# Two products at a time, token block by token block, where x is renewed, with other first loads and the first rotary on VectorE

## The chip, the cores and the metric

The kernel runs on one NeuronCore of a Trainium2 chip. TensorE multiplies into PSUM; VectorE, ScalarE and GpSimd do the rest; SyncE issues most DMAs, and ScalarE and GpSimd can issue some too. Each engine works through its own queue in program order and waits on semaphores. The metric is the device time of one execution in microseconds, the median of several runs.

## The reference, cut to what matters

Four layers run one after the other on the same x of 256 tokens by 1024 channels, all in float32: two layers of a first kind and then two of a second kind.

```python
def hybrid_layer(x, ...):             # layers one and two
    hdn = rms_norm(x, norm_w)
    qa, ka, va, za, qb, kb, vb, zb, ga, gb = split_cols(hdn @ w_in)   # 10 x 1024 columns
    ya = dilated_mixture(rope(qa), rope(ka), va) * silu(za)
    yb = rms_norm(diff_attention(rope(qb), rope(kb), vb)) * silu(zb)
    merged = sigmoid(ga) * (ya @ w_proj_a) + sigmoid(gb) * (yb @ w_proj_b)
    return x + merged @ w_out

x = rms_norm(x, final_norm_w)         # between layers two and three

def hybrid_layer_2(x, ...):           # layers three and four
    proj = rmsnorm(x, pre_mix_g) @ w_in
    ...                               # gated delta rule, windowed attention, two gates
    x = x + rmsnorm(mix, post_mix_g)
    ff = square(relu(rmsnorm(x, pre_mlp_g) @ w_ff1)) @ w_ff2
    return x + rmsnorm(ff, post_mlp_g)
```

## The kernel before

Tokens lie on partitions in two token blocks of 128 (`t` = 0, 1), channels in 8 blocks of 128 (`c`). A product of x with a weight of 512 columns needs x transposed: `to_lh` transposes four channel blocks on TensorE (tile `tp`), ScalarE copies them times the norm's gain into the high part `lhi`, and VectorE subtracts this from the product to make the low part `llo`. A weight comes in pieces of two channel blocks (`raw`, 128 x 1024 values, 512 KB): ScalarE copies it to the high part `hi` and VectorE makes the low part `lo` (`split_next`, lines 284 and 285). `mm3` then multiplies high by high, high by low and low by high: three matmuls for one channel block and one token block.

`proj` runs a product of 512 columns: by default channel block by channel block, both token blocks in turn; with `sweep=True` all 8 channel blocks for token block 0 and then all for token block 1, which keeps four pieces alive. `proj_w` is the same with the weight as the stationary side.

All weight pieces stand in one list in order of use (`stream`, filled by `plan1` and `plan2`). `raw` has three buffers (`NRAW`) and `hi` and `lo` four each (`NSPLIT`). `feed` splits the next piece when one of the four is released (`release`, after its last matmul) and asks for the load of the next raw piece behind it. The loads are issued by SyncE; a load waits there until VectorE has made the low part of the piece that had the buffer.

The order on every engine is written out by hand with a clock: one unit of `clk` is two calls of `mm3`. After each `mm3`, `tick(0.5)` calls `feed`, moves the clock on and issues what is due; `at(k, fn)` puts work off by k units. So a number such as the lag of `normed` says behind which matmul an instruction stands.

x is renewed at the end of each layer. In layers one and two this is the product with `w_out`, two column halves (`g` = 0, 1), both with `sweep=True`: `out_evac` adds the result to x (line 805). After layer two it also makes both norms at once (the final norm and the next layer's first): squares on ScalarE, the fold with the final gain on VectorE (line 816), factors on GpSimd (`both`), then `normed` (line 583) and `to_lh`; `own` scales x itself. In layers three and four the second matrix of the MLP adds up 8 blocks `fc` of the hidden width in PSUM (`back`); the last block goes token block by token block, and `post` and `update` (lines 857 to 873) make the norm, add to x and call `then`, which norms x for the next layer. The layers of the second kind begin with a gate of 512 columns (`silu_gate(0, True)`) and a small product of 272 columns (`small`), whose pieces are 128 x 544.

At the start x and the first pieces are loaded, the first gain is turned into columns (`norm_columns`), and `prepare` transposes x for layer one. `turned` copies query or key tiles out of PSUM, turns 16 of every 64 columns (`rope`, four instructions on GpSimd, lines 427 to 430) and `flip` transposes the tile.

## Time and profile before

| | |
|---|---|
| median of 3 runs | 1742.82 us (1741.65 to 1745.22) |
| profiled execution, its own time | 1741.27 us |
| its span, first to last instruction | 1739.5 us |
| TensorE busy | 1705.6 us, 98% |
| VectorE busy | 1169.9 us, 67% |
| ScalarE busy | 996.4 us, 57% |
| GpSimd busy | 268.1 us, 15% |
| read from HBM | 270.53 MB, 156 GB/s over the span |

PE is TensorE's matmuls, PEld its weight loads, DVE VectorE, ACT ScalarE, POOL GpSimd, SP SyncE; a q behind an engine's name means its sequencer, which issues DMAs. A tile is named by what is written and what is read (`lo<-raw,hi`). The duration of one matmul covers its pipeline, so the next one starts before it ends: rows that name several matmuls tell the pace better. PEclk is the share of TensorE's full clock that was granted. In a row of a stretch the last two numbers are the share of time in which the 16 DMA engines were busy and the GB/s that they moved.

### The profile page before, as it was taken

The page shows a single profiled execution, that of the slowest core. Times are in us where ns is not written, and L with a number is a line of the kernel's source. Part 1 is how long each engine was busy: PE and PEld are TensorE (multiplying, and loading weights), DVE is VectorE, ACT ScalarE, POOL GpSimd, SP SyncE. Part 2 cuts the span into 40 slices and gives each one's busy share as a digit, 9 for nine tenths or more (in the row PEclk, how much of TensorE's full clock was granted, in tenths as well). Part 3 has the DMA queues.
Part 4 walks back from the last instruction along what each step waited for, and adds up shares of the span by engine and source line. Part 5 has one row for each costly group of instructions (what it writes and reads, how often), then busy time and mean ns, then how long its engine had stood idle before and what let it go on. Part 6 is the DMA issues. An engine that isn't in the chain of part 4 may idle for free.

```text
span 1739.5 us, 26865 instructions
## 1 busy us (share of the span) xinstructions
PE 1705.6 (98%) x9865; PEld 1484.6 (85%) x9865; DVE 1169.9 (67%) x2189; ACT 996.4 (57%) x1786; POOL 268.1 (15%) x507
## 2 busy tenths in 40 slices
PE   8999999999999999999999999999999999999998
PEld 6788888888888888898889889998998888889997
DVE  5676776666777766788585676555788584775554
ACT  6666665466666654665665455445565666464443
POOL 2112321031123200320220000000320210010000
PEclk9999999999999999999999999999999999999999
DMA  6655465466655565554332655665554333646564
GB/s 206 196 173 167 152 189 173 159 195 181 177 164 155 172 192 174 168 166 134 96 104 86 197 167 182 194 193 170 160 170 140 87 102 93 198 158 195 184 184 140
DMA packets 158932, 282.27 MB, mean 162 GB/s; under 512 B 20560, under 2 KB 28496, under 8 KB 158800
## 3 DMA queue, kind: packets, MB, share of 16 engines
q1 hardware_dynamic: 157840, 277.83, 53.0%
q0 software_dynamic: 720, 2.62, 0.4%
q8 instruction: 78, 1.28, 0.3%
q14 instruction: 54, 0.44, 0.1%
q10 hardware_dynamic: 240, 0.09, 0.0%
HBM read 270.53 MB, written 1.59 MB: 156 GB/s over the span
## 4 chain that ended last, share of the span: by engine, by line
PE 51%; DVE 5%; issue 1%; ACT 1%; POOL 0%; DMA 0%; DVEq 0%; POOLq 0%; SPq 0%; ACTq 0%
PE acc L314 6%; PE acc L312 6%; PE acc L313 6%; PE acc L353 5%; PE acc L354 5%; PE acc L355 5%; PE facc L313 3%; PE facc L312 3%; PE facc L314 3%; DVE lo L285 2%; DVE hcv L993 1%; PE inv L1177 1%; PE inv L1167 1%; PE tp L371 1%; PE pt L507 1%
## 5 line engine op out<-in xcount | busy, mean ns | idle before, releaser
L285 DVE TENSOR_TENSOR lo<-raw,hi 128x1024 fp32r<-128x1024 f32 (+1 forms) x504 | 617.3, 1231 | 343.9 <-ACT hi L284 328.1
L284 ACT ACTIVATE hi<-raw 128x1024 fp32r<-128x1024 f32 (+1 forms) x504 | 527.3, 1052 | 357.5 <-PE acc L314 149.0
L312 PE MATMUL acc<-hi,lhi 128*128 128x512 f32 (+1 forms) x1344 | 550.4, 410 | 1.2 <-ACT lhi L385 1.2
L314 PE MATMUL acc<-hi,llo 128*128 128x512 f32 (+1 forms) x1344 | 526.2, 392 | 0.4 <-DVE llo L388 0.3
L313 PE MATMUL acc<-lo,lhi 128*128 128x512 f32 (+1 forms) x1344 | 524.2, 390 | 0.6 <-DVE lo L285 0.5
L314 PEld LDWEIGHTS acc<-hi,llo 128*128 128x128 f32 x1344 | 253.5, 189 | 57.4 <-DVE llo L388 3.4
L313 PEld LDWEIGHTS acc<-lo,lhi 128*128 128x128 f32 x1344 | 255.3, 190 | 41.3 <-DVE lo L285 2.0
L312 PEld LDWEIGHTS acc<-hi,lhi 128*128 128x128 f32 x1344 | 255.0, 190 | 39.7 <-ACT lhi L385 1.4
L353 PE MATMUL acc<-lhi,hi 128*128 128x256 f32 x832 | 239.1, 287 | 0.0
L355 PE MATMUL acc<-lhi,lo 128*128 128x256 f32 x832 | 235.4, 283 | 0.0
L354 PE MATMUL acc<-llo,hi 128*128 128x256 f32 x832 | 235.4, 283 | 0.0
L353 PEld LDWEIGHTS acc<-lhi,hi 128*128 128x128 f32 x832 | 159.5, 192 | 1.2 <-issue 0.4
L354 PEld LDWEIGHTS acc<-llo,hi 128*128 128x128 f32 x832 | 159.5, 192 | 0.7
L355 PEld LDWEIGHTS acc<-lhi,lo 128*128 128x128 f32 x832 | 159.4, 192 | 0.0
L312 PE MATMUL facc<-hi,fh 128*128 128x512 f32 x256 | 99.8, 390 | 0.0
L313 PE MATMUL facc<-lo,fh 128*128 128x512 f32 x256 | 99.8, 390 | 0.0
L314 PE MATMUL facc<-hi,fl 128*128 128x512 f32 x256 | 99.6, 389 | 0.0
L509 ACT ACTIVATE ptS<-pt 128x384 f32<-128x384 f32 x80 | 39.2, 490 | 82.0 <-PE pt L507 81.8
L546 POOL TENSOR_SCALAR pf<-pss 128x1 f32<-128x1 f32 x8 | 3.7, 458 | 467.6 <-ACT pj L860 467.6
L500 DVE CUSTOM_DVE_ANT_0 s<-sc,tab 128x256 f32<-128x256 f32 x192 | 60.4, 352 | 11.2 <-PE sc L496 10.6
L993 DVE SCALAR_TENSOR_TENSOR hcv<-acc,cw,hcv 128x255 f32<-128x255 f32 (+1 forms) x144 | 58.2, 475 | 1.5 <-ACT hcv L990 1.4
L314 PEld LDWEIGHTS facc<-hi,fl 128*128 128x128 f32 x256 | 48.1, 188 | 10.1
(306 smaller groups left out, 2206.9 us busy)
## 6 DMA issues: line engine op xcount, KB each, us to landing
raw<-in_w_in_dram SPq DMA_DIRECT2D x272, 512.0 KB, 3.8
raw<-in_w_ff_dram SPq DMA_DIRECT2D x128, 512.0 KB, 4.4
raw<-in_w_proj_a_dram SPq DMA_DIRECT2D x16, 512.0 KB, 3.9
raw<-in_w_proj_b_dram SPq DMA_DIRECT2D x16, 512.0 KB, 3.7
raw<-in_w_out_dram SPq DMA_DIRECT2D x16, 512.0 KB, 3.7
raw<-in_w_up_sw_dram SPq DMA_DIRECT2D x16, 512.0 KB, 3.7
raw<-in_w_up_dn_dram SPq DMA_DIRECT2D x16, 512.0 KB, 3.7
raw<-in_w_o_dram SPq DMA_DIRECT2D x16, 512.0 KB, 3.8
```

The costliest lines, as they stand in the source:

```text
L284: S.activation(hi[:, :, :o], raw[:, :, :o], AF.Copy)
L285: V.tensor_tensor(out=lo[:, :, :o], in0=raw[:, :, :o], in1=hi[:, :, :o].bitcast(F32), op=ALU.subtract)
L312: T.matmul(a, lh[0][:, c, sl], hi[:, cc, :n], start=first, stop=False)
L313: T.matmul(a, lh[0][:, c, sl], lo[:, cc, :n], start=False, stop=False)
L314: T.matmul(a, lh[1][:, c, sl], hi[:, cc, :n], start=False, stop=last)
L353: T.matmul(a, hi[:, c % 2, sl], lh[0][:, c, :], start=(c == 0 and m % 2 == 0), stop=False)
L354: T.matmul(a, hi[:, c % 2, sl], lh[1][:, c, :], start=False, stop=False)
L355: T.matmul(a, lo[:, c % 2, sl], lh[0][:, c, :], start=False, stop=(c == 7 and m % 2 == 1))
L371: T.transpose(p[:, a, :], src[:, a * 128:(a + 1) * 128], ident)
L500: V.tensor_tensor_reduce(s[:, a:b], sc[:, a:b], bias[:, a:b], 1.0, FMIN, ALU.add, ALU.max, accum_out=mx[:, j:j + 1])
L509: S.activation(r, pt, AF.Copy)
L993: V.scalar_tensor_tensor(ha[:, m, d:], a[:, m, :256 - d], tap(3 - d, m), ha[:, m, d:], op0=ALU.mult, op1=ALU.add)
```

## The change

1. `proj_pair` runs two products at a time: all channel blocks of both for token block 0, then of both for token block 1. It serves the two halves of the output product of layer two, and the gate and the small product at the start of layers three and four. The last two blocks of the MLP's second matrix run in the same way (`back_last`).
2. Eight pieces are alive in such a pair, so four of them get a place of their own (`HOMES`): tiles of other stages that are free then. A piece with such a home doesn't count against the four `hi` and `lo` buffers; `feed` leaves at least `PACE` = 1.4 clock units between two splits when three pieces already wait.
3. The lags of `normed` go from 1.8 to 3.2 and 3.6 (layer two) and from 1.1 to 3.5 and 4.2 (layer three), and two calls of `pump` at the ends of these layers go.
4. At the start the second half of the first token block is loaded from ScalarE's queue, the first piece in two loads, and seven pieces are asked for at once, four of them into tiles of later stages. The first x columns are transposed ahead of the first split, and the first piece is split in halves.
5. The rotary of the first query and key tiles of layer one goes to VectorE.

```diff
+PACE = 1.4
+HOMES = {1: ("qk", "qk", "tok", "R"), 2: ("qk", "qk", "tok", "tg")}
...
-    def x_load(t, h=None):
+    def x_load(t, h=None, queue=nc.sync):
         c = slice(0, DM) if h is None else slice(512 * h, 512 * h + 512)
-        nc.sync.dma_start(X[:, t, c], I["x"][0, t * 128:(t + 1) * 128, c])
+        queue.dma_start(X[:, t, c], I["x"][0, t * 128:(t + 1) * 128, c])
...
-    count = {"raw": 0, "split": 0, "done": 0, "free": 0}
-    def plan(W, *segs):
+    count = {"raw": 0, "split": 0, "own": 0, "done": 0, "free": 0, "at": -9.0}
+    owns = deque()
+    def plan(W, *segs, homes=(None,) * 4):
         for k in range(0, 8, 2):
-            stream.append((W, k, segs))
-    def load_next():
-        W, k0, segs = stream[count["raw"]]
+            stream.append((W, k, segs, homes[k // 2]))
+    def load_next(home=None, rows_apart=False):
+        W, k0, segs, _ = stream[count["raw"]]
         count["raw"] += 1
-        raw = wp.tile([128, 2, 512], F32, name="raw", tag="raw", bufs=NRAW)
+        if home is None:
+            raw = wp.tile([128, 2, 512], F32, name="raw", tag="raw", bufs=NRAW)
+        else:
+            raw = act.tile([128, 2, 512], F32, name="raw", tag=home, bufs=2)
         o = 0
         for c0, n in segs:
-            nc.sync.dma_start(raw[:, :, o:o + n],
-                              W[k0 * 128:(k0 + 2) * 128, c0:c0 + n].rearrange("(c p) n -> p c n", p=128))
+            for c in ((0, 1), (1, 2)) if rows_apart else ((0, 2),):
+                nc.sync.dma_start(raw[:, c[0]:c[1], o:o + n],
+                                  W[(k0 + c[0]) * 128:(k0 + c[1]) * 128, c0:c0 + n].rearrange("(c p) n -> p c n", p=128))
             o += n
         raws.append((raw, o))
 
-    def split_next():
+    def split_next(rows_apart=False):
         raw, o = raws.popleft()
+        home = stream[count["split"]][3]
         count["split"] += 1
-        hi = wp.tile([128, 2, 512], F32R, name="hi", tag="hi", bufs=NSPLIT)
-        lo = wp.tile([128, 2, 512], F32R, name="lo", tag="lo", bufs=NSPLIT)
-        S.activation(hi[:, :, :o], raw[:, :, :o], AF.Copy)
-        V.tensor_tensor(out=lo[:, :, :o], in0=raw[:, :, :o], in1=hi[:, :, :o].bitcast(F32), op=ALU.subtract)
+        count["at"] = clk[0]
+        owns.append(home is None)
+        if home is None:
+            count["own"] += 1
+            hi = wp.tile([128, 2, 512], F32R, name="hi", tag="hi", bufs=NSPLIT)
+            lo = wp.tile([128, 2, 512], F32R, name="lo", tag="lo", bufs=NSPLIT)
+        elif home == "qk":
+            both = act.tile([128, 2, 2, 512], F32R, name="hl", tag="qk", bufs=2)
+            hi, lo = both[:, 0], both[:, 1]
+        else:
+            hi, lo = [act.tile([128, 2, 512], F32R, name=n, tag=home, bufs=2) for n in ("hi", "lo")]
+        for c in (slice(0, 1), slice(1, 2)) if rows_apart else (slice(0, 2),):
+            S.activation(hi[:, c, :o], raw[:, c, :o], AF.Copy)
+            V.tensor_tensor(out=lo[:, c, :o], in0=raw[:, c, :o], in1=hi[:, c, :o].bitcast(F32), op=ALU.subtract)
...
-        while count["split"] < len(stream) and count["split"] < count["free"] + NSPLIT:
+        while count["split"] < len(stream):
+            if stream[count["split"]][3] is None:
+                if count["own"] >= count["free"] + NSPLIT:
+                    break
+            if len(splits) >= NSPLIT - 1 and clk[0] - count["at"] < PACE:
+                break
...
-        count["done"] += 1
+        count["done"] += owns.popleft()
...
+    def proj_pair(lh, evacs):
+        accs, pieces = [acc2() for _ in evacs], {}
+        for t in range(2):
+            for j, evac in enumerate(evacs):
+                for c in range(8):
+                    if t == 0 and c % 2 == 0:
+                        pieces[j, c // 2] = piece()
+                    hi, lo, n = pieces[j, c // 2]
+                    mm3(accs[j][t], n, lh, c, t, hi, lo, c % 2, c == 0, c == 7)
+                    if t and c % 2:
+                        release()
+                    if c == 7:
+                        evac(accs[j][t], t)
+                    tick(0.5)
...
-        G.tensor_tensor(out=a, in0=x[:, :, 0:16], in1=tbl(cc, 0, 16), op=ALU.mult)
-        G.tensor_tensor(out=b[:, :, 0:8], in0=x[:, :, 8:16], in1=tbl(ss, 0, 8), op=ALU.mult)
-        G.tensor_tensor(out=b[:, :, 8:16], in0=x[:, :, 0:8], in1=tbl(ss, 8, 16), op=ALU.mult)
-        G.tensor_tensor(out=x[:, :, 0:16], in0=a, in1=b, op=ALU.add)
+        E.tensor_tensor(out=a, in0=x[:, :, 0:16], in1=tbl(cc, 0, 16), op=ALU.mult)
...
             for g in range(2):
-                plan(A, (base + 512 * g, 512))
+                homes = HOMES[1] if l == DEPTH - 1 and g == 0 and A.tensor is I["w_out"].tensor else (None,) * 4
+                plan(A, (base + 512 * g, 512), homes=homes)
     def plan2(l):
         W = I["w_in_2"][l]
         plan(W, (3072, 512))
-        plan(W, (4096, 16), (5136, 256))
+        plan(W, (4096, 16), (5136, 256), homes=HOMES[2])
...
         for fc in range(8):
-            for k, g in ((0, 0), (0, 1), (2, 0), (2, 1)) if fc < 7 else ((0, 0), (2, 0), (0, 1), (2, 1)):
-                stream.append((W2, 4 * fc + k, ((512 * g, 512),)))
+            for i, (k, g) in enumerate(((0, 0), (0, 1), (2, 0), (2, 1)) if fc < 6 else ((0, 0), (2, 0), (0, 1), (2, 1))):
+                stream.append((W2, 4 * fc + k, ((512 * g, 512),), HOMES[2][i] if fc == 6 else None))
...
             q, k = qk_tile([8, 256], F32R), {}
-            proj(lh, into_stack(q, r, rope1)[1], sweep=first)
-            proj(lh, into_keys(k, r, rope1))
+            E = V if first and l == 0 else G
+            proj(lh, into_stack(q, r, rope1, E)[1], sweep=first)
+            proj(lh, into_keys(k, r, rope1, E))
...
                     c = vcol["pre_mix_g_2"]
-                    normed(t, rn, vT[:, c:c + 8], 1.8, xf)
+                    normed(t, rn, vT[:, c:c + 8], (3.2, 3.6)[t], xf)
...
-        for g in range(2):
-            proj(lm, out_evac(g), sweep=True)
-        if l == DEPTH - 1 and not last:
-            pump(clk[0] + 0.3)
+        if l < DEPTH - 1:
+            for g in range(2):
+                proj(lm, out_evac(g), sweep=True)
+        else:
+            proj_pair(lm, [out_evac(g) for g in range(2)])
...
-        def silu_gate(g, sweep=False):
+        def silu_gate(g):
             szs.append(t4k("sz"))
-            proj(lh, into_silu(szs[g], None, dnng[:, 128 * l:128 * l + 128]), sweep=sweep)
-        silu_gate(0, True)
-        proj(lh, small)
+            proj(lh, into_silu(szs[g], None, dnng[:, 128 * l:128 * l + 128]))
+        szs.append(t4k("sz"))
+        proj_pair(lh, [into_silu(szs[0], None, dnng[:, 128 * l:128 * l + 128]), small])
...
-            if fc < 7:
-                for pc in range(2):
-                    for g in range(2):
-                        hi, lo, n = piece()
-                        for cc in range(2):
-                            c = 2 * pc + cc
-                            for t in range(2):
-                                mm3(facc[t][g], 512, (fh, fl), c, t, hi, lo, cc, fc == 0 and c == 0, False)
-                                if t and cc:
-                                    release()
-                                tick(0.5)
-                return
+            for pc in range(2):
+                for g in range(2):
+                    hi, lo, n = piece()
+                    for cc in range(2):
+                        c = 2 * pc + cc
+                        for t in range(2):
+                            mm3(facc[t][g], 512, (fh, fl), c, t, hi, lo, cc, fc == 0 and c == 0, False)
+                            if t and cc:
+                                release()
+                            tick(0.5)
+        def back_last(facc):
             pieces = {}
             for t in range(2):
-                for g in range(2):
-                    for c in range(4):
-                        if t == 0 and c % 2 == 0:
-                            pieces[g, c // 2] = piece()
-                        hi, lo, n = pieces[g, c // 2]
-                        mm3(facc[t][g], 512, (fh, fl), c, t, hi, lo, c % 2, False, c == 3)
-                        if t and c % 2:
-                            release()
-                        if c == 3:
-                            post(facc[t], g, t, fss, gmlp, then, r2)
-                        tick(0.5)
+                for fc in (6, 7):
+                    for g in range(2):
+                        for c in range(4):
+                            if t == 0 and c % 2 == 0:
+                                pieces[fc, g, c // 2] = piece()
+                            hi, lo, n = pieces[fc, g, c // 2]
+                            mm3(facc[t][g], 512, hs[fc], c, t, hi, lo, c % 2, False, fc == 7 and c == 3)
+                            if t and c % 2:
+                                release()
+                            if fc == 7 and c == 3:
+                                post(facc[t], g, t, fss, gmlp, then, r2)
+                            tick(0.5)
...
                     rstd(rn[:, t:t + 1], nss[:, 2 * t:2 * t + 1], nss[:, 2 * t + 1:2 * t + 2])
-                    normed(t, rn[:, t:t + 1], vT[:, c:c + 8], 1.1)
+                    normed(t, rn[:, t:t + 1], vT[:, c:c + 8], (3.5, 4.2)[t])
...
-        for fc in range(8):
+        for fc in range(6):
             back(fc, facc)
-            if fc + 2 < 8:
-                hidden(fc + 2)
-        if not last:
-            pump(clk[0] + 0.9)
+            hidden(fc + 2)
+        back_last(facc)
...
+    x_load(0, 1, nc.scalar)
     norm_columns = column_load("norm_w")
-    x_load(0, 1)
-    load_next()
+    load_next(rows_apart=True)
...
-    load_next()
-    norm_columns()
-    split_next()
     x_load(1)
     load_next()
-    for t in range(2):
-        at(0.7 * t, lambda t=t: prepare(t, vT[:, vcol["norm_w"]:vcol["norm_w"] + 8], lag=2.6))
-    pump(0)
+    for home in ("sz", "sz", "tg", "tg"):
+        load_next(home)
+    norm_columns()
+    gain = vT[:, vcol["norm_w"]:vcol["norm_w"] + 8]
+    prepare(0, gain, (0,), 2.2)
+    split_next(rows_apart=True)
+    split_next()
+    prepare(0, gain, (1,), 2.3)
+    at(1.2, lambda: prepare(1, gain, lag=2.6))
     feed()
     tab_load("cc", "if")
     at(1.8, lambda: tab_load("ca", "ba"))
```

## Rows read from the trace of the kernel before

**Rows 1.** The page, part 1: busy time of TensorE, share of the span, instructions.

```profile
PE 1705.6 (98%) x9865; PEld 1484.6 (85%) x9865; DVE 1169.9 (67%) x2189; ACT 996.4 (57%) x1786; POOL 268.1 (15%) x507
```

**Rows 2.** List of waits, TensorE, whole trace: who, for whom, total us, times, longest.

```profile
PE tp L446 <- POOL tok L430: 4.0, 2, 3.6
```

**Rows 3.** List of waits, TensorE, from 698 to 712 us.

```profile
PE tp L371 <- DVE xn L583: 1.3, 2, 0.6
PE tp L371 <- DVE xf L583: 0.9, 1, 0.9
```

**Rows 4.** List of waits, TensorE, from 1214 to 1228 us.

```profile
PE tp L371 <- DVE xn L583: 3.1, 2, 1.9
```

**Rows 5.** Stretches: length; busy us of PE, PEld, DVE, ACT, POOL; clock; DMA share.

```profile
5.00:9.10 4.10, 2.43 (x12) 1.76 (x13) 1.94 (x5) 2.85 (x9) 0.00 (x0) 1.00 1.02 380
...
26.16:29.58 3.42, 3.42 (x10) 2.65 (x9) 1.51 (x3) 2.48 (x4) 1.01 (x3) 0.50 0.77 294
29.58:60.00 30.42, 28.79 (x134) 23.03 (x133) 20.14 (x46) 18.05 (x24) 5.58 (x10) 1.00 0.67 187
...
698.00:712.00 14.00, 11.85 (x58) 8.78 (x57) 12.07 (x26) 9.22 (x25) 4.50 (x8) 1.00 0.39 98
...
1217.40:1220.80 3.40, 3.40 (x12) 2.67 (x13) 3.31 (x8) 2.47 (x9) 1.99 (x2) 0.50 0.54 110
```

**Rows 6.** Timeline, TensorE, start: start us, us, instruction, idle before and releaser.

```profile
7.61 0.51 PE L312 MATMUL acc<-hi,lhi 128*128 128x512 f32 x1 [1.18 <-ACT lhi L385]
...
21.15 0.39 PE L314 MATMUL acc<-hi,llo 128*128 128x512 f32 x1
```

**Rows 7.** Timeline, GpSimd and VectorE around the first rotary.

```profile
18.39 0.24 POOL L569 TENSOR_SCALAR rstd<-root 128x1 f32<-128x1 f32 x1
...
20.33 3.75 DVE L285 TENSOR_TENSOR lo<-raw,hi 128x1024 fp32r<-128x1024 f32 x3 [3.03 <-ACT hi L284]
...
21.68 1.32 POOL L427 TENSOR_TENSOR ra<-tok,tab 128x128 f32<-128x128 f32 x1
...
28.54 0.46 POOL L427 TENSOR_TENSOR ra<-tok,tab 128x128 f32<-128x128 f32 x1 [3.48 <-ACT tok L440]
```

**Rows 8.** Groups by line, VectorE, 0 to 60 us: busy us, mean ns.

```profile
L164 DVE SCALAR_TENSOR_TENSOR lv<-lv 128x64 f32<-128x64 f32 x4 | 0.7, 221 | 0.0
```

**Rows 9.** Groups by line, VectorE, from 684 to 722 us.

```profile
L285 DVE TENSOR_TENSOR lo<-raw,hi 128x1024 fp32r<-128x1024 f32 x9 | 10.9, 1224 | 4.1 <-ACT hi L284 4.1
L388 DVE SCALAR_TENSOR_TENSOR llo<-tp,vT,lhi 128x128 fp32r<-128x128 f32 x16 | 4.5, 347 | 0.2 <-ACT lhi L385 0.2
...
L805 DVE TENSOR_TENSOR X<-acc,X 128x512 f32<-128x512 f32 x4 | 2.8, 688 | 1.5 <-PE acc L314 1.5
...
L583 DVE TENSOR_SCALAR xn<-X,rr 128x512 f32<-128x512 f32 x2 | 1.0, 484 | 0.9 <-POOL rr L547 0.9
```

**Rows 10.** Groups by line, ScalarE, from 684 to 722 us.

```profile
L284 ACT ACTIVATE hi<-raw 128x1024 fp32r<-128x1024 f32 x10 | 10.4, 1057 | 4.1 <-DMA raw<-in_w_out_dram 2.2 <-DMA raw<-in_w_in_dram 1.8
...
L540 ACT ACTIVATE junk<-X 128x512 f32<-128x512 f32 x6 | 3.8, 629 | 4.4 <-DVE X L805 3.1 <-DVE X L816 1.3
L284 ACT ACTIVATE hi<-raw 128x544 fp32r<-128x544 f32 x4 | 2.6, 659 | 2.4 <-PE acc L314 1.6 <-DMA raw<-in_w_in_dram 0.9
```

**Rows 11.** Timeline, VectorE and TensorE, second gated product of layer two.

```profile
668.07 1.22 DVE L285 TENSOR_TENSOR lo<-raw,hi 128x1024 fp32r<-128x1024 f32 x1
...
675.48 0.60 PE L371 MATMUL tp<-ident,tg 128*128 128x128 f32 x4
```

**Rows 12.** DMA issues, 700 to 709 us: count, KB each, us to landing.

```profile
raw<-in_w_in_dram SPq DMA_DIRECT2D x3, 256.0 KB, 3.1
raw<-in_w_in_dram SPq DMA_DIRECT2D x1, 512.0 KB, 3.9
```

**Rows 13.** Timeline, VectorE, splits of the small product's weights.

```profile
715.95 0.72 DVE L285 TENSOR_TENSOR lo<-raw,hi 128x544 fp32r<-128x544 f32 x1 [0.63 <-ACT hi L284]
...
718.78 3.00 DVE L285 TENSOR_TENSOR lo<-raw,hi 128x544 fp32r<-128x544 f32 x2
```

17 lines of the change are left out of this document (10 added, 7 removed).

## The prediction

> **What bounds the kernel now.** I read the page first: TensorE is busy 98% of the span [rows 1]. A change can therefore win only the moments in which TensorE stands still or runs slowly, and must not make new ones. The list of TensorE's waits says where they are. Two of its largest entries lie at the places that the change touches: 3.6 us for the first rotary product [rows 2], and the transposes that wait for the normed x, 2.2 us between layers two and three [rows 3] and 3.1 us between layers three and four [rows 4]. Next I cut the trace into stretches. After the 3.6 us wait TensorE was granted half its clock (1.2 instead of 2.4 GHz) for 3.4 us, and again at 1217.4 us, behind the longer wait of [rows 4]. At half clock 10 instructions took 3.42 us; the 134 of the next stretch took 28.8 us of busy time, 0.215 each, so the 10 would have needed 2.15 [rows 5]: a slow stretch costs about 1.3 us. Then I read the timelines around the four places, and in the passages the duration of each kind of VectorE instruction, because weights, gates and norms all pass through VectorE.
>
> **Start (first loads, first rotary).** TensorE idles 1.2 us before its first real product, which ends at 21.4 us [rows 6]; at the first flip of the query tile it idles the 3.6. The flip is late because the four rotary instructions run on GpSimd: the first takes 1.32 us while VectorE splits three weights from 20.33 us on, and only 0.46 later, beside an idle VectorE [rows 7]. VectorE has no such instruction of 128 elements here; the nearest are 0.22 us for 64 elements [rows 8] and 0.69 for 512 [rows 9]. Four cost between 0.9 and 2.8 us; I take 1.0, near the 64-element row. The change gives them to VectorE for the first query and key tiles of layer one. There they wait for ScalarE's copy, and behind them in VectorE's queue stands the low part of the next product's first weight, for which TensorE waits. I follow it: the factor is ready at 18.6 in the trace [rows 7], 17.7 if the start is 0.9 earlier (below); the copy of 512 columns and two squares take about 0.7 + 2 x 0.8, the high part 1.06 [rows 10], the low part 1.2 [rows 9]: 22.3. The first product then ends at 20.5, one set of transposes later it is 21.1 and the first matmul that needs no low part is over at 21.3. So the flip no longer waits (3.6 us and the slow stretch of 1.3 go) and 1.0 us comes back.
>
> The loads: seven weight pieces are asked for at once instead of three and then one for each freed buffer; the second half of x goes by ScalarE's queue, behind the identity; SyncE's queue is short of that issue and has the second token block ahead of the third weight. The DMA engines run full there anyway (share 1.02 from 5 to 9.1 us [rows 5]), so the other queue gets nothing. The rotary table is issued behind four more pieces; at the 380 GB/s of that stretch seven pieces of 0.52 MB and x are in by about 16 us, before the rotary at 18.4. What remains is that ScalarE copies the first x columns ahead of the first weight, which it now takes in halves: bounds 0 and the 1.2 of [rows 6]; I take 0.9, since the weight's 1.06 us stood ahead of all columns. Start: -3.6 - 1.3 + 1.0 - 0.9 = -4.8 us, bounds -6.1 and -2.6.
>
> **Layers two to three (684 to 720 us).** After the change both column halves of the output product run for token block 0, then for block 1, and the next layer does the same with its gate and its small product. x of block 0 is complete 10.3 us (48 matmuls of 0.215) before the layer ends instead of 5.2. But the split of the next weights is tied to buffers: the gate's four pieces may be split only as the second half's pieces are released, in the last 5.2 us, just where VectorE has block 0's norm too. I lay out its queue from the first release (time 0, 18 matmuls or 3.9 us before the layer's end) with the durations of [rows 9]: from 0.2 the fold of the previous half 0.69, two normings 0.96, a split 1.2, eight low copies 2.25, two splits 2.4, block 0's own scaling about 0.48 + 0.69, the last addition 0.69, its fold 0.69, the fourth split 1.2. That ends at 11.4. TensorE wants it at 9.7: 3.9 of the old layer, two sets of transposes at 0.6 [rows 11], six of eight blocks of the gate (3.9) and 0.7 of waiting for the first norming. A wait of 1.7 us. Behind it comes the ring of three raw tiles: the small product's third piece needs the tile that the gate's fourth frees at 11.4; its load is issued in two parts, and the larger lands 3.1 us after its issue [rows 12], not before 14.5; high part 0.66 [rows 10], low part 0.72 [rows 13], gate product 0.69, low part of the fourth piece 0.72: 17.3. Only then comes block 1's norming, issued behind these, 0.48; TensorE has been at its transposes since 14.1. That is 3.7. In all 0.7 + 1.7 + 3.7 = 6.1 against 2.2, or +3.9. The bounds are -2.2 (all covered) and +5.5. I take +3.5, since instructions in a full queue start a little closer than they last. The wait of 3.6 at the start was followed by half clock, the 0.9 of [rows 3] was not: +0.7 here, half of a slow stretch, since part of the slowed work waits anyway.
>
> Ahead of this the first output weights now go to tiles of their own and are split during the product before. Their third piece needs a raw tile that VectorE frees at 669.3 [rows 11]; 3.9 us to land [rows 12] and both parts make 675.4, and the gate evacuation queued behind (two of 0.69) ends at 676.8, where TensorE wants its transposes at 675.5 [rows 11]: up to +1.3. I take +0.5, as the split may miss that place by one step.
>
> **Layers three to four (1205 to 1231 us).** Before: 3.1 us [rows 4] and a slow stretch of 1.3, 4.4. After, by the same queue with the post-norm's scaling and update (also 128x512) for fold and addition: 1.5 at block 0's transposes, whose norming stands behind the first split, 1.6 before the small product's pieces, 1.8 at block 1's: 4.9, or +0.5; bounds -4.4 and +2.5. The last layer has no successor, and its last half ends as before.
>
> The pacing (1.4) touches nothing else: elsewhere a split is issued only when fewer than three are waiting, and keeps its place.
>
> **VectorE beside GpSimd.** Two splits of 128x544 took 3.00 us in the stretch of the gate's product on GpSimd, where one alone took 0.72 [rows 13]. The Trainium skill (SBUF — State Buffer, section Who interferes with whom) says that a VectorE instruction with two SBUF inputs and a GpSimd one that reads SBUF exclude each other for a whole instruction; the trace agrees. What it does to the time is rival (d).
>
> **Sum.** -4.8 + 3.5 + 0.7 + 0.5 + 0.5 = +0.4 us. The profiled execution took 1741.27 us (span 1739.5 and 1.8 around it), 1.6 below the median of 1742.82; I forecast 1742.
>
> **Rivals.** (a) The passages are covered as they look on TensorE alone: 10.3 us of matmuls over each norm chain. Then -4.8 - 2.2 - 4.4 = -11.4: 1730 to 1732. For it: block 0's chain, some six instructions of at most 0.8 us, is over before its place in the queue. Against: VectorE is busy 12.1 of the 14 us from 698 to 712 already [rows 5], and the pair asks it for eight splits in 8 us. (b) Slower: the ring of three raw tiles decides in both passages. With block 1's transposes at 3.7 and 3.6 us, half clock behind both and the whole lead-in: +3.9 + 1.3 + 1.3 + 0.5 + 1.8 + 1.3 - 4.8 = +5.3, 1746 to 1748. It decides from where passages and lead-in lose 8.3 us together. For it: loads of 3 to 4 us. Against: in the second passage the transposes stand two blocks later. (c) The start doesn't do what it says: on VectorE the rotary holds up the weights as long as GpSimd held the flip, and the start is worth 1 us: +4.2, 1746. Against: VectorE idled 3 us before its splits [rows 7]. (d) The gate's product on GpSimd, issued just ahead of the last splits and block 1's norming, holds them as in [rows 13], 3.00 - 1.44 = 1.6 us in each passage: +3.6, 1745. Against: that product may be over by the time the pieces land.
>
> **How the numbers follow.** A change under 0.2% (3.5 us) can't be told from none here. The forecast has 0.40, its own range 1738 to 1746 (0.34 within 0.2%, 0.03 on either side); (a) 0.32, faster; (b) 0.16, slower; (c) 0.06, 0.04 of it slower; (d) 0.06, half of it slower. Faster 0.35, same 0.39, slower 0.26. The range reaches to the middle of (a) and the end of (b): 1731 to 1748.
>
> **What would show it.** Right: no wait of the flip at 21 us and no half clock at 26; then a TensorE wait at block 1's transposes in both passages, with VectorE full in front of it and the small product's high parts waiting for DMA. Wrong: transposes without a wait (a), or a first key product later than 23 us (c).

## The result and the profile after

The changed kernel took 1753.83 us (median; 1750.45 to 1753.95) beside 1742.24 for the kernel before, a ratio of 1.006 with a 95% interval of 1.0041 to 1.0078: 11.6 us slower by the medians, 7 to 14 by the interval, and 9.2 in a second set of runs (below). That is outside the range of the forecast. The profiled execution took 1753.94 us. Its page, part 1, against [rows 1]:

```profile
PE 1708.5 (98%) x9865; PEld 1486.9 (85%) x9865; DVE 1170.7 (67%) x2206; ACT 996.5 (57%) x1787; POOL 257.6 (15%) x491
```

TensorE is busy 2.9 us longer with the same 9865 matmuls, and the span is 12.6 us longer: most of the loss is standing still. Where, the list of TensorE's waits tells, first of the start (0 to 75 us):

```profile
PE sc L537 <- DMA kl<-kl: 2.5, 1, 2.5
PE acc L337 <- ACT hi L303: 1.3, 1, 1.3
PE sc L536 <- DMA kh<-kh: 1.3, 1, 1.3
PE wk L149 <- DMA row<-in_norm_w_dram: 1.2, 1, 1.2
PE wk L1540 <- DVE cold L1536: 1.1, 1, 1.1
```

The 3.6 us of [rows 2] are gone, as forecast. In their place stand 1.2 us for the row of norm_w, 1.3 for the first weight, and 3.8 for the copies of the keys (kh, kl) into the other half of their partitions, where the kernel before had 1.6:

```profile
PE sc L496 <- DMA kl<-kl: 1.6, 1, 1.6
```

The passage from layers two to three, 655.7 to 748 us, against [rows 3]:

```profile
PE tp L412 <- DVE xn L624: 5.7, 2, 5.0
PE acc L338 <- DVE lo L304: 1.4, 1, 1.4
PE tp L412 <- DVE tg L574: 1.2, 1, 1.2
```

Layers three to four, 1203.3 to 1261.8 us, against [rows 4]:

```profile
PE tp L412 <- DVE xn L624: 3.5, 2, 2.1
PE acc L338 <- DVE hl L304: 0.8, 2, 0.4
PE facc L338 <- DVE lo L304: 0.7, 1, 0.7
PE acc L338 <- DVE lo L304: 0.4, 1, 0.4
```

Stretches of both kernels that hold the same matmuls (columns as in [rows 5]), before and then after:

```profile
655.00:740.00 85.00, 82.77 (x467) 71.23 (x467) 61.14 (x100) 47.23 (x85) 17.63 (x40) 1.00 0.54 169
1195.00:1250.00 55.00, 51.88 (x292) 45.09 (x291) 36.86 (x54) 31.42 (x64) 12.85 (x24) 0.97 0.52 151
```

```profile
655.70:748.00 92.30, 84.02 (x468) 73.12 (x467) 61.87 (x104) 47.13 (x85) 20.14 (x44) 0.98 0.52 156
1203.30:1261.80 58.50, 53.16 (x292) 45.37 (x291) 36.03 (x56) 31.60 (x65) 11.63 (x29) 0.97 0.53 152
```

The first passage is 7.3 us longer: idle 8.28 instead of 2.23, and 1.25 more busy. The second is 3.5 longer: idle 5.34 instead of 3.12, 1.28 more busy. Half clock stands behind the longest waits, at the start and in both passages:

```profile
56.00:62.80 6.80, 5.32 (x14) 4.38 (x15) 2.08 (x7) 2.85 (x4) 0.23 (x1) 0.50 0.81 229
718.18:721.58 3.40, 3.40 (x18) 3.40 (x17) 1.61 (x7) 2.18 (x8) 0.00 (x0) 0.50 0.54 154
1240.42:1243.82 3.40, 3.40 (x12) 2.91 (x11) 2.23 (x9) 2.20 (x10) 0.04 (x1) 0.50 0.42 137
```

In the first passage this stretch makes up the extra busy time. In the second it isn't: the kernel before has a stretch of 3.4 us at half clock there too [rows 5]. What adds busy time there is the edges of the waits, six of them over 0.3 us instead of two. One of them, of 0.40 us:

```profile
1232.72 0.29 PE L337 MATMUL acc<-hl,lhi 128*128 128x272 f32 x1
1233.41 0.39 PE L338 MATMUL acc<-hl,lhi 128*128 128x272 f32 x1 [0.40 <-DVE hl L304]
1233.64 0.29 PE L339 MATMUL acc<-hl,llo 128*128 128x272 f32 x1
1233.76 0.29 PE L337 MATMUL acc<-hl,lhi 128*128 128x272 f32 x1
```

These matmuls start 0.12 to 0.13 us apart when nothing waits. Here the one before the wait takes 0.29 besides the 0.40 and the one behind it 0.23, so that the wait costs 0.27 more than its length. If the others cost the same (an estimate from this one), four more waits make 1.1 of the 1.28. The same passage in two other runs, neither of which has half clock there, the start alone and then the changed kernel again (both below):

```profile
1192.36:1247.18 54.82, 50.63 (x292) 43.92 (x291) 36.61 (x56) 31.65 (x65) 13.74 (x26) 1.00 0.49 154
1200.73:1257.51 56.78, 51.82 (x292) 43.95 (x291) 35.76 (x56) 30.95 (x64) 13.63 (x29) 1.00 0.52 158
```

The pairs take 1.2 us more busy time here at the full clock as well.

Now VectorE in front of the 5.0 us wait, which ends at 717.9:

```profile
710.11 0.73 DVE L304 TENSOR_TENSOR hl<-raw,hl 128x544 fp32r<-128x544 f32 x1 [0.20 <-ACT hl L303]
711.02 0.72 DVE L304 TENSOR_TENSOR hl<-raw,hl 128x544 fp32r<-128x544 f32 x1 [0.18 <-ACT hl L303]
714.18 0.73 DVE L304 TENSOR_TENSOR lo<-raw,hi 128x544 fp32r<-128x544 f32 x1 [2.44 <-ACT hi L303]
714.82 0.68 DVE L448 SCALAR_TENSOR_TENSOR sz<-th,acc 128x512 f32<-128x512 f32 x1
715.66 1.82 DVE L304 TENSOR_TENSOR lo<-raw,hi 128x544 fp32r<-128x544 f32 x1 [0.15 <-ACT hi L303]
717.40 0.47 DVE L624 TENSOR_SCALAR xn<-X,rr 128x512 f32<-128x512 f32 x1
```

and ScalarE and GpSimd beside it:

```profile
713.49 0.66 ACT L303 ACTIVATE hi<-raw 128x544 fp32r<-128x544 f32 x1 [2.51 <-DMA raw<-in_w_in_dram]
```

```profile
708.90 1.18 POOL L868 TENSOR_SCALAR rr<-ssf 128x1 f32<-128x1 f32 x1 [13.27 <-ACT junk L581]
...
712.07 0.57 POOL L588 TENSOR_TENSOR rr<-rr,nhalf_c 128x1 f32<-128x1 f32 x1
...
715.64 1.26 POOL L451 TENSOR_TENSOR sz<-sz,bv_dn_norm_g 128x512 f32<-128x512 f32 x1 [2.47 <-issue]
```

The reader is to see that VectorE isn't full: it stands idle for 2.44 us, behind a split whose raw weight comes late from the ring of three tiles, while the norming of block 1, whose factor has been ready since 712.6, is queued behind that split and the next. The next takes 1.82 us instead of 0.73, beside the gate's product on GpSimd. The Trainium skill (SBUF — State Buffer, section SBUF: two separate sides) says that whichever starts first, a VectorE instruction with two SBUF inputs or a GpSimd one that reads SBUF, gets the port pair that they share for its whole instruction, and the other is blocked; the trace agrees: the product began at 715.64 for 1.26 us, the split at 715.66.

### The profile page after: what moved, and what is told of

Read it like the earlier page. It is cut to its first block, busy times and chain, and to the rows that moved or that the text cites. A ratio compares the mean times of both kernels' runs of the same rounds, so it can differ in the third digit from the quotient of the medians.

```text
span 1752.1 us, 26861 instructions
## 1 busy us (share of the span) xinstructions
PE 1708.5 (98%) x9865; PEld 1486.9 (85%) x9865; DVE 1170.7 (67%) x2206; ACT 996.5 (57%) x1787; POOL 257.6 (15%) x491
## 3 DMA queue, kind: packets, MB, share of 16 engines
q8 instruction: 78, 1.28, 0.3%
## 4 chain that ended last, share of the span: by engine, by line
PE 75%; DVE 11%; issue 5%; DMA 4%; ACT 3%; POOL 2%; SPq 0%; DVEq 0%; POOLq 0%; ACTq 0%
PE acc L337 13%; PE acc L339 13%; PE acc L338 13%; PE acc L394 4%; DVE lo L304 4%; PE acc L395 4%; PE acc L396 4%; PE facc L338 3%; PE facc L339 3%; PE facc L337 3%; ACT hi L303 1%; DVE hcv L1037 1%; PE tp L412 1%; PE pt L548 1%; PE inv L1221 1%
## 5 line engine op out<-in xcount | busy, mean ns | idle before, releaser
L304 DVE TENSOR_TENSOR lo<-raw,hi 128x1024 fp32r<-128x1024 f32 (+1 forms) x495 | 605.7, 1230 | 338.9 <-ACT hi L303 325.2
L303 ACT ACTIVATE hi<-raw 128x1024 fp32r<-128x1024 f32 (+1 forms) x495 | 518.8, 1054 | 353.1 <-PE acc L339 141.0
L337 PE MATMUL acc<-hi,lhi 128*128 128x512 f32 (+1 forms) x1320 | 543.3, 412 | 1.3 <-ACT hi L303 1.3
L338 PE MATMUL acc<-lo,lhi 128*128 128x512 f32 (+1 forms) x1320 | 517.9, 392 | 2.4 <-DVE lo L304 2.4
L339 PE MATMUL acc<-hi,llo 128*128 128x512 f32 (+1 forms) x1320 | 518.9, 393 | 0.4 <-DVE llo L429 0.4
L338 PEld LDWEIGHTS acc<-lo,lhi 128*128 128x128 f32 x1320 | 251.4, 190 | 43.5 <-DVE lo L304 4.7
L338 PE MATMUL facc<-lo,fh 128*128 128x512 f32 x240 | 93.8, 391 | 1.0 <-DVE lo L304 1.0
L337 PE MATMUL facc<-hi,fh 128*128 128x512 f32 x240 | 93.7, 390 | 0.0
L339 PE MATMUL facc<-hi,fl 128*128 128x512 f32 x240 | 93.4, 389 | 0.0
L338 PEld LDWEIGHTS facc<-lo,fh 128*128 128x128 f32 x240 | 45.1, 188 | 10.7 <-DVE lo L304 1.9
```

Of the source, the lines that this page charges most:

```text
L303: S.activation(hi[:, c, :o], raw[:, c, :o], AF.Copy)
L304: V.tensor_tensor(out=lo[:, c, :o], in0=raw[:, c, :o], in1=hi[:, c, :o].bitcast(F32), op=ALU.subtract)
L337: T.matmul(a, lh[0][:, c, sl], hi[:, cc, :n], start=first, stop=False)
L338: T.matmul(a, lh[0][:, c, sl], lo[:, cc, :n], start=False, stop=False)
L339: T.matmul(a, lh[1][:, c, sl], hi[:, cc, :n], start=False, stop=last)
```

## Experiments

Theory A: the paired passages lose by themselves, through the raw tiles; the start gains, and gives part of it back at the copies of the keys. Rivals: the start works in full (B), the loss is one of alignment (C), VectorE's order alone (E), full DMA engines (F), GpSimd's gate product (d). Times are medians in us; the ratio is to the kernel before on the same chip, and differences between runs of different chips are taken from each run's own column of before.

| run | this | before | ratio | 95% interval |
|---|---|---|---|---|
| start alone | 1739.03 | 1741.50 | 0.999 | 0.9981 to 0.9999 |
| pairs alone | 1753.24 | 1741.50 | 1.007 | 1.0057 to 1.0083 |
| rotary alone | 1740.19 | 1741.50 | 0.999 | 0.9982 to 0.9999 |
| loads alone | 1740.15 | 1741.50 | 0.9997 | 0.9988 to 1.0005 |
| pair at 2-3 | 1746.02 | 1741.15 | 1.0028 | 1.0018 to 1.0039 |
| pair at 3-4 | 1741.76 | 1741.15 | 1.0004 | 0.9996 to 1.0013 |
| early norm | 1747.81 | 1741.15 | 1.0037 | 1.0025 to 1.0050 |
| two raws more | 1742.37 | 1741.15 | 1.0004 | 0.9995 to 1.0014 |
| raws and norm | 1746.55 | 1741.73 | 1.0028 | 1.0018 to 1.0037 |
| row first | 1736.53 | 1741.73 | 0.9971 | 0.9960 to 0.9982 |
| twin, own queue | 1739.63 | 1741.73 | 0.9985 | 0.9976 to 0.9994 |
| all mends | 1745.91 | 1741.73 | 1.0030 | 1.0015 to 1.0044 |
| changed again | 1751.61 | 1742.45 | 1.0055 | 1.0038 to 1.0072 |
| pairs again | 1752.65 | 1742.45 | 1.0063 | 1.0049 to 1.0078 |
| raws and row | 1740.86 | 1742.45 | 0.9996 | 0.9986 to 1.0007 |
| late gate | 1747.27 | 1741.15 | 1.0036 | 1.0023 to 1.0050 |

The second table is worked out from the traces: the matmuls of each are numbered in order of time, and the end of the matmul that stands at the time in the heading in the kernel before is subtracted from the end of the one with the same number. It shows where one execution loses or wins. The two rows of the pairs alone are one kernel, as are the two of the changed one: they differ by up to 2.9 and 4.4 us in a column. A small difference between two rows says little; what is gained or lost within one row, over a passage, says more.

```
before, us         15     54     65    230    655    740   1195   1250   1725
changed         +1.96  -3.49  +1.38  +0.59  +0.73  +8.00  +8.26 +11.78 +12.98
changed again   +2.84  -2.59  -0.10  -0.88  -1.11  +5.99  +5.73  +7.51  +8.61
start alone     +2.35  -3.10  -3.55  -4.41  -4.35  -4.12  -2.64  -2.82  -3.07
rotary alone    +0.36  -4.31  -0.68  -1.50  -1.42  -1.08  -1.02  -0.28  -0.46
loads alone     +2.14  -1.99  -2.10  -0.78  +0.38  +0.61  +0.80  +0.59  +1.11
row first       -0.04  -5.20  -4.79  -5.65  -5.55  -5.53  -5.52  -5.72  -4.48
twin, own queue +1.66  -3.80  -3.61  -2.74  -2.36  -2.16  -0.86  -1.04  -1.44
pairs alone     -0.58  +1.27  +1.12  +0.20  +0.30  +7.02  +6.98 +11.53 +12.43
pairs again     +1.51  -1.26  -1.49  -1.04  +0.35  +7.33  +7.26  +9.13  +9.55
pair at 2-3     +2.37  -3.06  -3.58  -4.45  -4.45  +4.07  +3.84  +5.11  +5.59
pair at 3-4     +2.78  -2.68  -0.66  -1.54  -1.51  -1.43  -1.68  +2.46  +3.12
early norm      +1.71  -3.72  -3.69  -4.54  -4.48  +1.16  +1.10  +3.49  +4.39
two raws more   +1.50  -3.93  -1.99  -2.85  -2.82  -0.94  -0.94  -0.20  +1.14
raws and norm   +2.17  -3.27  -3.12  -3.93  -3.87  +1.11  +0.97  +1.42  +2.64
raws and row    +0.12  -5.29  -4.94  -5.69  -5.92  -4.37  -2.95  -2.05  -0.89
all mends       +0.19  -5.27  -4.68  -4.62  -4.54  +0.08  +0.02  +1.78  +2.29
late gate       +1.76  -3.66  -2.77  -2.90  -3.07  +3.32  +3.19  +7.12  +8.43
```

**Start or passages?** Start alone puts the passages back (pairs alone puts back the start block and the first rotary's engine). Cut from its edit:

```diff
-            proj_pair(lm, [out_evac(g) for g in range(2)])
+            for g in range(2):
+                proj(lm, out_evac(g), sweep=True)
...
-        back_last(facc)
```

> The kernel before with the new first loads and the first rotary on VectorE, and no paired products. Theory A (the start's gain is given back at the waits for the copies of the keys, and the passages alone make the change slower): within 1.5 us of before, with a wait of about 2.5 us for kl near 57 us. Rival B (the start works as forecast and all of the loss is in the passages, which then cost about 16 us): 4 to 5 us faster than before.

> The kernel before with the paired products at both passages (their homes, pace and lags too), and the old first loads and first rotary on GpSimd. Theory A: 10 to 12 us slower than before, with the waits of the changed kernel at 678, 700, 710, 718, 1223, 1233 and 1239 us about as long as they were. Rival B: 15 to 17 us slower. Rival C (the two parts act on each other, through the alignment of the half-clock stretches): 5 us or less.

The passages lose it all: 11.7 us, as A says. The start wins 2.5 (by the interval 0.2 to 3.3), less than B and more than A. A put the give-back at 57 us in every execution; this one has 1.2 us for kl and no half clock. One passage put back at a time. In the first of the two runs the last two blocks of the MLP stay paired (`back_last`); only the lag of `normed`, the gate and the small product of layer four go back:

> The changed kernel with the layers three-to-four passage put back as it was before (its products one after the other, lags of 1.1, no homes there); the paired products at the layers two-to-three passage and the start stay. Theory A (each passage loses by itself, 7 to 8 us with the lead-in at two to three, 3.5 at three to four, and the start gives 0 to 3 us): 4.5 to 7.5 us slower than before. Rival C (the loss is one of alignment between the stretches, not of the single passages): it doesn't split, within 2 us of either kernel.

> The changed kernel with the layers two-to-three passage put back as it was before (the products one after the other, lag 1.8, no homes there); the paired products at layers three to four and the start stay. Theory A: 0.5 to 3.5 us slower than before. Rival C: it doesn't split, within 2 us of either kernel.

Both lie where A has them: 4.9 and 0.6 us, with the start's gain in each. The 0.6 alone would fit C too, within 2 us of before; the 4.9 doesn't, and C falls. Without the start's 2.5 the passages cost 7.3 and 3.1 in the medians, 10.4 together beside 11.7 and 10.2 for the pairs alone. In the second table the first passage (655 to 740) costs 8.5, with 6.8 us of half clock instead of 3.4, and the second (1195 to 1250) 4.1, in an execution 2.3 us above its run's median. The paired last blocks that stay in the first of these runs still cost 1.3 at 1195 to 1250, so the split between the passages is a rough one.

**The start.** Either half of it alone:

```diff
-            E = V if first and l == 0 else G
+            E = G
```

> The kernel before with only the first rotary on VectorE. Theory A (the copies of the keys are bound by the transfers that fill the DMA engines, whoever issues them earlier): 1.5 to 3 us faster, the flip's wait of 3.6 us gone and the half clock at 26 us with it, part given back as a longer wait for kl near 55 us. Rival D (it is the new loads that make the copies late): 4 to 5 us faster, with the wait for kl as before, 1.6 us.

> The kernel before with only the new first loads (second half of X on ScalarE's queue, rows apart, four raw tiles more), the rotary on GpSimd. Theory A (norm_w's row lands later behind X's second half, its wait of 1.2 us and the longer half clock after it): 1 to 2 us slower at the end of the first product; the flip still waits about 3 us; 0 to 2 us slower in all. Rival D: 3 us or more slower.

The rotary alone is 4.3 us ahead at 54 us and has lost 3.6 of it by 65, in waits of 1.2 for kh and 2.2 for kl and half clock behind them: D, which laid the late copies to the new loads, falls. The loads alone were a surprise: 1.4 us faster in the median (the interval includes no change) where 0 to 2 slower was expected. With the rotary on GpSimd the first flip doesn't wait at all, and only the second does, 1.1 us at 30.6. GpSimd and VectorE in that run, against [rows 7]:

```profile
20.40 0.46 POOL L468 TENSOR_TENSOR ra<-tok,tab 128x128 f32<-128x128 f32 x1 [0.51 <-ACT tok L481]
...
21.50 0.46 POOL L471 TENSOR_TENSOR tok<-ra,rb 128x128 f32<-128x128 f32 x1
...
22.52 3.50 DVE L304 TENSOR_TENSOR lo<-raw,hi 128x1024 fp32r<-128x1024 f32 x3 [4.37 <-ACT hi L303]
```

The rotary now runs ahead of VectorE's three splits, 20.40 to 21.96 us, and not beside them, and the first product ends 2.1 us later than before. So the new loads remove the wait that the rotary was moved for, and the gains of the two halves don't add. Next, norm_w's row ahead of the second half of x on ScalarE's queue:

```diff
-    x_load(0, 1, nc.scalar)
     norm_columns = column_load("norm_w")
+    x_load(0, 1, nc.scalar)
```

> The changed start alone (as in the run with the start alone), with norm_w's row issued on ScalarE's queue ahead of the second half of X. If the row's place in the queue is what made the first product late: the wait of 1.3 us at 6.2 us goes, TensorE is 1 us or more earlier at 15 us than with the start alone, and the time is 0.5 to 1.5 us less. If the raws or the splits decide anyway: the same time, with a longer wait for hi at 8 us.

The row's first timeline lines on TensorE, start alone and then with the row first, and a wait that is new there:

```profile
6.17 0.20 PE L149 MATMUL wk<-ident,row 16*128 16x16 f32 x1 [1.25 <-DMA row<-in_norm_w_dram]
...
8.71 0.53 PE L337 MATMUL acc<-hi,lhi 128*128 128x512 f32 x1 [1.31 <-ACT hi L303]
```

```profile
4.85 0.28 PE L149 MATMUL wk<-ident,row 16*128 16x16 f32 x1
...
7.22 0.63 PE L412 MATMUL tp<-ident,X 128*128 128x128 f32 x4 [1.43 <-DMA X<-in_x_dram]
7.61 0.47 PE L337 MATMUL acc<-hi,lhi 128*128 128x512 f32 x1
```

2.4 us earlier at 15 us and 2.7 in the time, more than expected. The wait for the row went; one of 1.4 us for the second half of x, now behind the row, takes the place of the 1.3 for hi, and the first product still begins 1.1 us earlier. The half clock behind it lasted 3.4 us instead of 6.8. The intervals of the two runs just overlap, but the three executions with the row first stand at -0.04 to +0.19 us at 15 us, the nine with the start unmended at +1.50 to +2.84. This is the best version of all, 5.2 us (3.1 to 7.0) faster than before. Last, the first copies of the keys from ScalarE's queue ("twin, own queue" in the tables; one of the two lines, that of kl is changed alike; `queue` is ScalarE's for the first key tiles and SyncE's after them):

```diff
...
-                        nc.sync.dma_start(st["kh"][b, i:8:2, :].bitcast(F32), st["kh"][a, i:8:2, :].bitcast(F32))
+                        queue.dma_start(st["kh"][b, i:8:2, :].bitcast(F32), st["kh"][a, i:8:2, :].bitcast(F32))
...
```

> The changed start alone, with the first four copies of the keys issued from ScalarE's queue and not SyncE's. If they come late because they stand behind the raw loads in SyncE's queue: they land in 4 us or less after their issue, the waits for kh and kl near 57 us go, and TensorE is 4 to 5 us ahead of before at 65 us, in all runs; 0.5 to 2 us faster than the start alone. If the DMA engines' share is what they lack: landing as before, 4 to 7 us, and no difference in time, or slower by the issues on ScalarE.

They landed 3.9 to 4.7 us after their issue (4.2 to 5.2 in the run of the start alone), and the time stayed. The queue isn't what they lack; that it is the share of the DMA engines is argued and not shown. DMA from 48 to 52 us (the queue's packets, MB and share of the 16 engines; then copies, KB each, us from issue to landing), the changed kernel and then the start alone:

```profile
q1 hardware_dynamic: 710, 1.08, 100.3%
...
kh<-kh SPq DMA_DIRECT2D x2, 256.0 KB, 6.4
kl<-kl SPq DMA_DIRECT2D x2, 256.0 KB, 7.4
```

```profile
q1 hardware_dynamic: 791, 1.12, 98.7%
...
kh<-kh SPq DMA_DIRECT2D x2, 256.0 KB, 4.3
kl<-kl SPq DMA_DIRECT2D x2, 256.0 KB, 4.9
```

Up to some 660 us both programs are the same, in the order of every queue; the DMA engines are full in both, and the copies land 2.1 to 2.5 us apart. Why, no run shows.

**The passages.** Norming earlier:

```diff
-                    normed(t, rn, vT[:, c:c + 8], (3.2, 3.6)[t], xf)
+                    normed(t, rn, vT[:, c:c + 8], (3.2, 1.2)[t], xf)
...
-                    normed(t, rn[:, t:t + 1], vT[:, c:c + 8], (3.5, 4.2)[t])
+                    normed(t, rn[:, t:t + 1], vT[:, c:c + 8], (3.5, 1.7)[t])
```

> The changed kernel with the norming of token block 1 issued earlier at both passages, so that on VectorE it stands ahead of the small product's last two splits (layers two to three) and of its last (three to four). Theory A (the ring of three raw tiles: what is late is the small product's raws, and the norming only stands behind them): the wait for xn of 5.0 us at 718 shrinks to under 1, and a wait for the low part of the small product's fourth split of 3 to 4 us takes its place; 0 to 2.5 us faster than the changed kernel. Rival E (only the order on VectorE was wrong): 5 to 7 us faster than the changed kernel, with no wait of over 1 us left at 718.

Two tiles more, in a buffer (LT) that is free in both passages:

```diff
+        if len(segs) == 2 and k0 < 4:
+            if k0 == 0:
+                big.append(act.tile([128, 2, 2, 512], F32, name="raw2", tag="LT", bufs=1))
+            raw, home = big[-1][:, k0 // 2], "LT"
...
-            while count["raw"] < len(stream) and len(raws) < NRAW:
+            while count["raw"] < len(stream) and sum(h != "LT" for *_, h in raws) < NRAW:
```

> The changed kernel with two more raw tiles at each passage, for the first two pieces of the small product, in memory that is idle then; orders on the engines unchanged. Theory A: the DMAs of the small product's pieces are issued 3 to 4 us earlier, the waits for low parts at 710 and 1233 to 1236 go, the wait for xn at 718 falls from 5.0 to 1 to 2 us, and the half clock behind it goes or shortens; 4 to 7 us faster than the changed kernel. Rival E: the wait at 718 stays over 3.5 us, at most 2 us faster. Rival F (the DMA engines are full there, and more tiles only queue longer): landing times stay, within 1 us of the changed kernel.

Norming earlier saves 1.6 us of the first passage and 1.1 of the second (5.6 instead of 7.3, 2.4 instead of 3.5), the tiles 5.4 and 2.8 (1.9 and 0.7). The idle time of the first passage falls from 8.3 to 5.7 and 4.4; with the norming 6.8 us of half clock follow, with the tiles none. In medians, each against before, that is 2.5 to 5 us below the changed kernel's two for the norming and 8 to 10 for the tiles, more than was expected of the tiles and up to twice what was expected of the norming; the part that is not in the passages is the scatter of the start (second table, 230 us). With the tiles the whole kernel is level with before, the start's gain included: the ring is the larger cause, E and F fall. Waits, 655 to 740 us, and ScalarE at the third piece, with two tiles more:

```profile
PE tp L417 <- DVE xn L629: 1.7, 2, 1.0
PE acc L343 <- DVE lo L309: 1.4, 1, 1.4
PE tp L417 <- DVE tg L579: 1.3, 1, 1.3
```

```profile
707.14 0.65 ACT L308 ACTIVATE hi<-raw 128x544 fp32r<-128x544 f32 x1
```

ScalarE no longer waits for that load, and the wait of 5.0 is 1.0. With the early norming that wait stood at 2.2 us; theory A had it under 1, with a longer wait for the fourth split in its place, and that was wrong. Both mends together:

> The changed kernel with both mends of the passages: two raw tiles more for the small product, and the norming of block 1 issued earlier. Theory A (after the raws, what still waits at block 1's transposes is the norming behind the splits): 1 to 3 us faster than with the raws alone, 0 to 2.5 us faster than the kernel before; no wait over 1 us for xn at block 1. Rival G (the paired order costs by itself, through the wait for tg in the lead-in and the narrow matmuls, so that it can't come out ahead): 0 to 2 us slower than before.

A miss: 4.8 us slower than before, 3.6 more than the tiles alone. Waits, 655 to 740 us:

```profile
PE tp L417 <- DVE xn L629: 2.9, 2, 2.2
PE tp L417 <- DVE tg L579: 1.4, 1, 1.4
PE acc L343 <- DVE lo L309: 1.4, 1, 1.4
```

Of the 3.1 us that the first passage loses against the tiles alone, 1.4 is idle time, and the rest goes with 3.4 us of half clock at 708.3, which the tiles alone don't have. The wait is 2.2 again, as with the early norming alone, where VectorE's norming waited 0.46 us for the factor from GpSimd (0.93 with both mends):

```profile
707.40 0.49 DVE L624 TENSOR_SCALAR xn<-X,rr 128x512 f32<-128x512 f32 x1 [0.46 <-POOL rr L588]
```

The transposes stand ahead of the small product's last blocks on TensorE, which would have covered that chain once their weights were there. The lag of 3.6 is the better one for a passage with its weights in time (a wait of 1.0 against 2.2). Block 0's product of gate and gain on GpSimd, issued 4.5 clock units later, behind block 1's norming, in the changed kernel:

> The changed kernel with block 0's product of gate and gain on GpSimd issued later, behind block 1's norming, at both passages; nothing else is moved. Rival (d) of the prediction (GpSimd's product holds VectorE's splits): the fourth split takes 0.7 us in both passages, block 1's transposes come 1.1 and 0.6 us earlier, 1 to 2 us faster than the changed kernel. Theory A (the ring decides): most of the wait stays, 3.5 us or more at 718, and still 8 us or more slower than before. If the fourth split's time isn't GpSimd's doing: 1.82 us as before, and no difference.

The fourth split takes 0.72 us at both places and the waits for xn fall from 5.0 to 4.1 and from 2.1 to 1.6: rival (d) is real, at 0.5 to 0.9 us a passage, and most of the wait stays. The kernel is still 6 us slower than before, where A expected 8; how much of its distance to the changed kernel's median is this edit, the overlapping intervals leave open.

**Together.**

> Both mends of the passages and norm_w's row first, on the changed kernel. If the parts add up: 1 to 4 us faster than before, that is 1737 to 1741; level with the start alone or up to 1 us better.

> The changed kernel itself, beside the pairs alone on the same chip. If the start's gain is there: 1.5 to 4 us faster than the pairs alone, 8 to 10 us slower than before. If the late copies of the keys eat it every time: within 1 us of the pairs alone, and again waits for kh and kl of over 3 us in sum near 55 us.

> The pairs alone once more, as the other side of that comparison: 11 to 13 us slower than before.

> The changed kernel with two raw tiles more for the small product at each passage and norm_w's row first; norming as in the changed kernel. If the parts add up (raws took the passages to about 1 us slower than before, the start with the row first gives 5 us): 3 to 5 us faster than before only if the passages cost under 2 us; by the sum of the two runs 1739 to 1741, and so behind the start with the row first and no pairs, 1736.5. If the pairs pay once their raws are there: 1736 or less.

All mends carry the early norming and its loss with them: 4.2 us slower, where 1 to 4 faster was expected. The pairs again cost 10.2, a little less than the 11 to 13 expected. The changed kernel again is 1.0 us below the pairs, with intervals that overlap, so the start's gain beside the pairs is between the two cases; its waits for kh and kl sum to 2.3 us this time. The tiles with the row first come out as the sum of the single runs said, 1.6 us faster than before (the interval includes no change) where the row first without pairs is 5.2 faster: mended so, the pairs still cost 3.6 us. In the trace that is 1.6 and 0.9 us in the passages and 1.0 behind 1700 us; the 1.4 lost between 740 and 1195 is 10.2 us of half clock instead of 3.4, as in the start alone, where the passages are the old ones. The tiles without the row cost the same beside the start alone, 3.7 us. So the pairs save nothing with these mends. The waits of the lead-in (1.0 to 1.4 us) and for the gate's fourth low part (1.3 to 1.4) stand in all these runs, and no run mends them: that the paired order can't come out ahead at all (rival G) isn't shown.

## Why the prediction was wrong

**What bounds the kernel**: right. The losses are moments in which TensorE stood still or was granted half its clock, and the edges of waits, which the forecast counted as nothing: 0.27 us at the wait of 1233 us.

**Start, -4.8**: -2.5 in the medians. The flip's wait and its slow stretch went. The rotary took VectorE 0.9 us for 1.0 forecast (0.29 + 0.22 + 0.22 + 0.29, overlapping), but the sum's +1.0 was not lost on TensorE, which didn't wait for it. Two steps failed. "The other queue gets nothing" left out what that queue held: norm_w's row behind 256 KB of x, so that the first product ended 2.0 us late, not 0.9 early; with the row first it came out level. What the loads give by themselves was missed too: they alone end the collision of the rotary with the splits. And the step didn't ask what is late next: the copies of the keys, issued 2.9 us earlier than before, into full DMA engines. The gain stood at 2.6 to 3.9 us at 54 us in each of the nine profiled executions that have this start unmended; at 65 us it was anything from 3.7 to a loss of 1.4, by when the copies landed and whether half clock followed.

**Layers two to three, +3.5 and +0.7, lead-in +0.5**: 7.3 in the profiled execution. The waits were laid out as 0.7, 1.7 and 3.7, and were 0.7, 1.4 and 5.0: the mechanism (raw tile, load, high part, low part, then the norming) was right step by step, the last wait 1.3 too small, of which 0.9 went with the late gate: the fourth split beside the gate's product, which was kept apart as rival (d). The lead-in (the wait for tg) took 1.2 of its bound of 1.3, not 0.5, and the half clock all of its price, not half. Each doubt was decided in the change's favour, "since instructions in a full queue start a little closer than they last": VectorE's queue wasn't full but waited for loads.

**Layers three to four, +0.5**: 3.5. The waits, forecast as 1.5, 1.6 and 1.8, were 1.4, 1.1 and 2.1, with 0.7 before them in the last blocks of the old layer: 0.4 more in all. Two terms were put at nothing. One is the half clock behind the new wait, 1.3 us; it came at 1240.4 us, though not in every execution: the changed kernel again lost 1.8 here and has none. The other is the busy time that four more waits add at their edges, 1.2 to 1.3 us, in both executions. The price of the old slow stretch was itself overlapped: without it the same old passage took as long (54.8 us in the start alone, 54.9 before), with 4.2 us idle instead of 3.1.

**The pacing** "touches nothing else" held with the new start, where the order of every queue is that of the start alone up to some 660 us, but not with the old one: in the pairs alone it put one weight load behind a table's at 13.6 us.

**The last layer** "ends as before" didn't hold: 0.7 us, a wait for a low part of 0.4 us and what follows.

**Rivals.** (a) fell: nothing was covered. (b) is what happened. Its passages and lead-in came to 10.1 us, and the pairs alone cost 11.7 and 10.2. Its sum failed on the start that it shared with the forecast, -4.8 where -2.5 was measured. (c) fell as a mechanism, since VectorE's splits waited for ScalarE's high parts and not for the rotary, but the start did give less than forecast. Its sign, a first key product later than 23 us, came (23.67), and misled: TensorE reached it without a wait, late from the norm_w row. (d) is a part of (b)'s last wait. So the largest error of the forecast's sum is the passages with their lead-in, 5.2 for 10 to 12: the wait for the ring of raw tiles taken too short (3.7 for 5.0), its half clock at half price or none, the lead-in at 0.5 for 1.2.

## What to carry to other kernels

Pairing products to hide a chain of norms asks twice the weights of the same few microseconds: count the tiles between a load's issue and the split that frees its tile before counting TensorE's cover. A wait that is removed is worth nothing until the next late thing has been named; here that was a copy in full DMA engines, and of two edits against one wait only one pays: with the new loads the first rotary ran ahead of the splits even on GpSimd. Each further wait also costs its edges. A small row that everything waits for goes first on its queue: that one moved line was worth 2.4 us in the trace and 2.7 in the medians, about as much as the whole start.

## What the hardware showed unexpectedly

The same copies, issued by the same program at the same place, landed 4.3 and 6.4 us after their issue in two executions, at full DMA share in both. A wait of 2.1 us in the second passage was followed by half clock in one execution of the changed kernel (1240.4 us) and by none in another, and so it was in the two runs of the pairs alone (1239.1 us, and none). And GpSimd is held by VectorE's splits as well as holding them: its addition of two columns took 1.18 us at 708.90, beside a split from 708.69 to 709.91, against 0.30 in the kernel before.

```profile
705.45 0.30 POOL L825 TENSOR_SCALAR rr<-ssf 128x1 f32<-128x1 f32 x1 [5.24 <-ACT junk L540]
```
